# Attention stage of a hybrid encoder: values loaded with a unit's scores, first loads by halves of the channels, branch products from the first tail slot on

## The chip, the cores and the metric

The kernel runs on one core of one Trainium2 chip. What is compared is the device time of one execution in microseconds. TensorE is called PE in the profile, VectorE DVE, ScalarE ACT, GpSimd POOL, SyncE SP; PEld is TensorE's load of the stationary operand.

## What is computed

One pre-norm encoder layer over two inputs: 2048 tokens of a sample and 1024 tokens of a prompt, 1024 channels, fp32.

```python
h = _rms_norm(x, norm_g)
qkv_a, z_a, qkv_b, z_b, beta, alpha, gate_a, gate_b = jnp.split(h @ w_in, split_points, -1)
q_a, k_a = _rms_norm(q_a, q_norm_g), _rms_norm(k_a, k_norm_g)
o_a = _neighbourhood_attention(q_a, k_a, v_a, rpb) * jax.nn.silu(z_a)   # 8 heads of 64
o_b = _deltanet_branch(qkv_b, z_b, beta, alpha, ...)                    # 4 heads of 128
merged = sigmoid(gate_a) * (o_a @ w_branch_a) + sigmoid(gate_b) * (o_b @ w_branch_b)
return x + merged @ w_out
```

The attention is two-dimensional: a token sits on a grid 64 wide, and attends to a window of 8 rows by 16 columns, with a learned bias by relative position. The DeltaNet branch is a chunked recurrent scan in both directions.

## The kernel before, in words

Most products are made in fp16 by splitting each fp32 operand into a high and a low half (`whi`, `wlo`, `rh`, `rl`, `ph`, `pl`) and adding three products (or, where the values `vw` hold both halves, two).

*DeltaNet stage* (`deltanet`, to about 1717 us). All projections but those of q, k and v of the attention are made here, as a filler of 128x256 fp16 products between the steps of the scan. The work goes slot by slot: `step_slot` runs the scan's steps and lets `fill(u)` add filler products until TensorE's count in this slot, `T.cost`, reaches a quarter, a half, three quarters and all of `UNITS`; a 256-wide fp16 product counts 1. At the end the last chunk's outputs are stored (`obd<-P`).

*Attention stage* (to about 2342 us). Its first loads are the weights `w.hi`, `w.lo` of the first pair of heads and the normalised tokens `H[4]` (tiles `rh4`, `rl4`, in two halves of the tokens), from DRAM tiles that the first stage wrote; `load_H` loads a block. Four pairs of heads follow one another; each has six blocks of 512 tokens (two of the prompt, 4 and 5, then four of the sample), and each block four slots. In a slot, `slot(mm)` interleaves a projection of 128 tokens (24 products `ppn`, 128x384, made piece by piece through `work(n, mm)`, with the pieces of `PW`) with one unit of the attention, which is 128 queries by 12 or 16 rows of keys. A unit goes through the slots as a pipeline:

- `unit_bias`: every fourth unit loads the bias `bt` by eight loads for each head (`bias_tile`; POOL's memset comes first).
- `unit_scores` at the end of slot n: products `pS`; DVE adds `bt` and takes the maximum (`Sb`). `unit_exp` follows on ACT in slot n+1.
- `unit_transpose` and `unit_low` in slot n+2, for each of two heads: transposes `pT`, high half `ph` on ACT, low half `pl` on DVE. For the first head the values `vw` are loaded here, by three or four DMAs of 64 KB out of `w.vd`, a DRAM tile; there are two buffers of `vw`.
- `unit_values` in slot n+3: products `pon` out of `vw`, `ph` and `pl`; then `unit_out` on ACT and `unit_sum` on DVE.
- after four units `block_out`: transposes `pO`, gate `otn`, store `oad`.

The projection's values go the other way: `proj_parts` makes `vt`, `norm` stores it to `w.vd` (`vd<-vt`), and `proj_tr` transposes q and k (`pqk`) and writes the high and low halves of the keys, `kh` and `kl`, one tile for the sample (2048 keys) and one for the prompt (1024, two buffers).

*Tail* (13 slots, 2342 to 2432). The projections are over and the last units run. From its second slot on the filler of `slot` is `two_chunks`: the products of two chunks of the branch outputs with the branch weights, `py_` (128x256, 24 of them to one PSUM tile, tag "g", two buffers), made by `merged`. `gated` (DVE, `th<-th,py`) frees the PSUM tile; `split` makes the halves `mm`. `begin` sets up a chunk by six steps in later slots (its second argument gives the slot of each): loads, scaling, `x` times `z` on POOL (the step "act" is next after the load; the steps are `dma`, `act`, `dve2`, `pe`, `dve2`, `dve2`), and so on. What is left of the two chunks is made by `run_merged` when the tail is over.

*Output stage* (to 2876 us). The other chunks' `py_` and the output products `po_`.

What sets the order: in the attention stage and the tail TensorE, DVE and ACT run in the order of the program text (`Pinned`, `PIN = 7`). The order on SP, which issues all loads and stores one after the other, and on POOL is the planner's: it takes the instruction that its model finds ready, by priorities that come from the order in which the program emits them. An instruction that waits holds up what is behind it on its engine. All operations carry line 61, a helper; so they are told apart by the names of their tiles.

Of the kernel before, what the change touches and what calls it, by code (L numbers as in the profile page):

```python
# [45 lines left out]
def emit(nc, tc, x_prompt, x_sample, norm_g, w_in, attn_q_norm_g, attn_k_norm_g, attn_rpb, dn_conv_w, dn_a_log,  # L46
# [120 lines left out]
    def deltanet():  # L167

        SLOTS, UNITS, MOST, FIRST, LAST = 7, 34.0, 3000, (0, 4), (3, 5)
        sm = opn("sm", bufs=4)
        dcp = opn("dcp")
        wdp = opn("wdp", bufs=8)
# [1326 lines left out]
    def proj_tr(w, b, t2):  # L1501

        pt = ps_Q.tile([128, 2, 256], F32, name="pqk", tag="Q")
        for j in range(2):
            x = w.sq.pop(0)
            TP.transpose(pt[:, 0].rearrange("p (b r c) -> p r b c", b=4, r=4)[:, 2 * j:2 * j + 2], x[:, 0:128], ident)
            TP.transpose(pt[:, 1, 128 * j:128 * j + 128], x[:, 128:256], ident)

        if t2 == 0:
            w.q[b] = tuple(nk.tile([128, BLK], F16, name=n, bufs=5) for n in ("qh", "ql"))  # L1510
        sq = 0 if b < 4 else 1
        if sq not in w.k:
            w.k[sq] = tuple(nk.tile([128, (2048, 1024)[sq]], F16, name=f"{n}{sq}", bufs=(1, 2)[sq]) for n in ("kh", "kl"))
        qh, ql = w.q[b]
        kh, kl = w.k[sq]
        qv = lambda t: t.rearrange("p (b r) -> p b r", b=4)[:, :, 64 * t2:64 * t2 + 64]
        pq_ = pt[:, 0].rearrange("p (b r) -> p b r", b=4)
        bs = slice(BLK * (b - 4 * sq) + 256 * t2, BLK * (b - 4 * sq) + 256 * t2 + 256)

        def high():  # L1520
            SP.activation(qv(qh), pq_, AF.Identity, scale=gg)
            SP.activation(kh[:, bs], pt[:, 1], AF.Copy)

        def low():
            VP.scalar_tensor_tensor(qv(ql), in0=pq_, scalar=gg, in1=qv(qh), op0=MUL, op1=SUB)
            VP.tensor_tensor(kl[:, bs], pt[:, 1], kh[:, bs], op=SUB)
            nonlocal done
            done += 1

        at(0, "act2", high)  # L1530
        at(0, "dve2", low)
# [8 lines left out]
    def unit_scores(u):  # L1540


        w, b, cb = u.w, u.b, u.cb
        rt = types[b]
        u.nr = 16 if rt == 1 else 12
        u.kr = row0[b] - (0 if rt == 0 else 4)
        u.kc = min(max(16 * cb - 8, 0), 32)
        if cb == 0:
            w.Os = wk.tile([128, 4, 128], F32, name="Os")
        u.Os = w.Os  # L1550
        rows0, N = 32 * (b // 4), 32 * u.nr
        qg, kg = w.q[b], [t.rearrange("p (r c) -> p r c", c=64) for t in w.k[b // 4]]
        pS = [ps_S.tile([128, 512], F32, name="pS", tag="S") for _ in range(2)]
        for n, (a, c) in enumerate(((0, 0), (0, 1), (1, 0))):
            for hd in range(2):
                hs = slice(64 * hd, 64 * hd + 64)
                TP.matmul(pS[hd][:, 0:N], qg[a][hs, 128 * cb:128 * cb + 128],
                          kg[c][hs, u.kr - rows0:u.kr - rows0 + u.nr, u.kc:u.kc + 32], start=(n == 0), stop=(n == 2))
        u.Sb = [wk.tile([128, 512], F32, name="Sb", bufs=SBB) for _ in range(2)]
        mx = sm.tile([128, 2], F32, name="mx")  # L1560
        for hd in range(2):
            VP.tensor_tensor_reduce(out=u.Sb[hd][:, 0:N], in0=pS[hd][:, 0:N], in1=w.bts[hd][:, (0, 1, 1, 2)[cb], :], scale=1.0,
                                    scalar=-3e38, op0=ADD, op1=MAX, accum_out=mx[:, hd:hd + 1])
        u.nm = sm.tile([128, 2], F32, name="nm")
        VP.tensor_tensor(u.nm, mx, npq.to_broadcast([128, 2]), op=MUL)
# [8 lines left out]
    def unit_transpose(u, hd):  # L1574

        w, N = u.w, 32 * u.nr
        if hd == 0:
            u.vw = wk.tile([128, 4, 256], F16, name="vw")
            for j in range(u.nr // 4):
                SY.dma_start(u.vw[:, j, :], w.vd[u.kr + 4 * j:u.kr + 4 * j + 4, u.kc:u.kc + 32, :])  # L1580
            u.ph = [wk.tile([128, 512], F16, name="ph", bufs=PHB) for _ in range(2)]
            u.pl = [wk.tile([128, 512], F16, name="pl", bufs=PHB) for _ in range(2)]
            u.pT = [None, None]
# [68 lines left out]
                SY.dma_start(H[b][i][:, :, HB * j:HB * j + HB], hdr[b][:, i, j])  # L1652

    w = pair(0)
    for i, t in enumerate((w.hi, w.lo)):
        SY.dma_start(t.rearrange("p j k c -> p (j k c)"), wt0[:, 3072 * i:3072 * i + 3072])
    w.p = [abp[:, 4 + j:5 + j] for j in range(3)]
    pair_scales(w, V)
    load_H(4)
    load_H(5)  # L1660

    order = [10, 11, 8, 9, 0, 1, 2, 3, 4, 5, 6, 7]
# [243 lines left out]
    for hp_ in range(4):  # L1906
# [5 lines left out]
        for b, ats in ((4, ()), (5, (5, 4)), (0, ()), (1, (0,)), (2, (1,)), (3, (2, 3))):  # L1912
            if hp_ == 3 and b == 0:
                branch_weights(0)
            for t in range(4):
                if hp_ == 3 and b == 2 and t == 2:
                    begin(order[0], (0, 2, 3, 4, 4, 5))
                mm = proj_mm(w, b, t)
                slot(mm)
                work(1, mm)  # L1920
# [7 lines left out]
                    units.append((sn + LA, u))  # L1928
    close(p_mm)
    p_g, ps_g = pool("p_g", bufs=2, side="right", space=PSUM)  # L1930
    begin(order[1], (0, 2, 4, 5, 5, 6))

    def two_chunks():
        yield from merged(cs_[0], nwm)
        yield from merged(cs_[1], wkm)

# [2 lines left out]
    while units or B or C or later:  # L1939
        if ws is None and done == 48:  # L1940
            early()
        if n == 11:
            begin(order[2], (0, 2))
        slot(filler if n else iter(()))
        n += 1
    while stk:
        close(stk.pop())
# [67 lines left out]
```

## Time and profile before

| | us |
|---|---|
| three runs | 2873.61, 2874.6, 2876.13 |
| median | 2874.6 |
| the profiled execution | 2877.91 |
| its span | 2876.1 |
| busy: PE, PEld, DVE, ACT, POOL | 2714.3, 2159.7, 1794.1, 1397.0, 890.1 |

In all views times are microseconds from the start of the span. "Busy" is the time in which an engine executes; a bracket behind an instruction gives the idle time ahead of it on its engine and what ended it. A wait for several things is put down to the one that came last by the profile; where the named one has been done for long, it was another, often a load. The clock column is the granted clock of TensorE as a share of 2.4 GHz. SPq is SyncE's issue of a DMA.

### The profile page before, as it was taken

The page shows a single profiled execution, that of the slowest core. Times are in us where ns is not written, and L with a number is a line of the kernel's source. Part 1 is how long each engine was busy: PE and PEld are TensorE (multiplying, and loading weights), DVE is VectorE, ACT ScalarE, POOL GpSimd, SP SyncE. Part 2 cuts the span into 40 slices and gives each one's busy share as a digit, 9 for nine tenths or more (in the row PEclk, how much of TensorE's full clock was granted, in tenths as well). Part 3 has the DMA queues.
Part 4 walks back from the last instruction along what each step waited for, and adds up shares of the span by engine and source line. Part 5 has one row for each costly group of instructions (what it writes and reads, how often), then busy time and mean ns, then how long its engine had stood idle before and what let it go on. Part 6 is the DMA issues. An engine that isn't in the chain of part 4 may idle for free. (4 is left out here: it accounts for less than half of the span.)

```text
span 2876.1 us, 64811 instructions
## 1 busy us (share of the span) xinstructions
PE 2714.3 (94%) x24902; PEld 2159.7 (75%) x24902; DVE 1794.1 (62%) x4266; ACT 1397.0 (49%) x3861; POOL 890.1 (31%) x1545
## 2 busy tenths in 40 slices
PE   7889999989899999999999989999999988999999
PEld 6778888978788878888788885666666656666675
DVE  7567767577574758746666523566666657556654
ACT  4445455555445545555455543666666654212211
POOL 2222111221111212112212215445444433554543
PEclk9899999999999999999999999999999989999999
DMA  7433443344532443232435747333333454543341
GB/s 255 131 112 91 120 122 86 108 128 129 131 105 83 134 135 110 81 89 71 134 106 164 201 138 202 110 102 92 103 90 93 136 191 163 199 147 130 133 155 66
DMA packets 486931, 364.97 MB, mean 127 GB/s; under 512 B 144227, under 2 KB 449247, under 8 KB 485727
## 3 DMA queue, kind: packets, MB, share of 16 engines
q1 hardware_dynamic: 486623, 360.84, 42.0%
q8 instruction: 196, 3.21, 0.5%
q14 instruction: 112, 0.92, 0.1%
HBM read 262.53 MB, written 98.20 MB: 125 GB/s over the span
## 5 line engine op out<-in xcount | busy, mean ns | idle before, releaser
L61 PE MATMUL pp<-hh,w 128*128 128x256 f16 x6912 | 1214.2, 276 | 21.7 <-DVE thz L61 10.1
L61 PEld LDWEIGHTS <-w 128*128 128x128 f16 x10368 | 1021.8, 99 | 159.0 <-issue 16.9
L61 PE MATMUL pp<-hl,w 128*128 128x256 f16 x3456 | 955.5, 276 | 1.7 <-DMA hl<-hdr 1.1
L61 PE MATMUL ppn<-whi,rh 128*128 128x384 f16 x768 | 253.5, 330 | 5.6 <-DMA rh<-hdr 5.6
L61 PEld LDWEIGHTS <-y 128*128 128x128 f16 x2304 | 225.6, 99 | 43.6 <-DVE th L61 8.7
L61 PE MATMUL ppn<-whi,rl 128*128 128x384 f16 x768 | 253.8, 331 | 0.7 <-DMA rl<-hdr 0.7
L61 PE MATMUL ppn<-wlo,rh 128*128 128x384 f16 x768 | 253.1, 330 | 0.0
L61 PEld LDWEIGHTS <-rh 128*128 128x128 f16 x1536 | 146.0, 99 | 77.0 <-issue 9.3
L61 ACT ACTIVATE thz<-pp,wfc 128x256 f32<-128x256 f32 x288 | 124.3, 472 | 158.3 <-PE pp L61 110.0
L61 POOL TENSOR_TENSOR th<-th 128x128 f32<-128x128 f32 (+1 forms) x240 | 149.0, 638 | 165.0 <-DVE th L61 146.7
L61 PEld LDWEIGHTS <-mm 128*128 128x128 f16 x1008 | 98.6, 98 | 115.2
L61 ACT ACTIVATE mm<-th 128x256 f16<-128x256 f32 x144 | 59.1, 446 | 227.7 <-POOL th L61 223.6
L61 DVE TENSOR_TENSOR pl<-pT,ph 128x384 f16<-128x384 f32 (+1 forms) x192 | 111.0, 599 | 88.6 <-ACT ph L61 87.6
L61 DVE CUSTOM_DVE_ANT_0 Sb<-pS,bt 128x384 f32<-128x384 f32 (+1 forms) x192 | 108.9, 599 | 74.8 <-PE pS L61 32.2
L61 ACT ACTIVATE vn<-pk,nbeg 128x128 f32<-128x128 f32 x176 | 64.8, 368 | 171.0 <-PE pk L61 169.9
L61 POOL TENSOR_TENSOR rqk<-rqk,mhalf 128x4 f32<-128x4 f32 x48 | 51.1, 1065 | 305.6 <-DVE rqk L61 303.3
L61 DVE SCALAR_TENSOR_TENSOR S<-S,egl,pk 128x128 f32<-128x128 f32 x160 | 54.8, 343 | 137.5 <-PE pk L61 113.2
L61 ACT ACTIVATE Sb<-Sb,nm,pq 128x384 f32<-128x384 f32 (+1 forms) x192 | 140.0, 733 | 0.4 <-DVE nm L61 0.3
L61 ACT ACTIVATE Os<-pon,rsn 128x64 f32<-128x64 f32 x192 | 49.9, 311 | 181.0 <-PE pon L61 181.0
L61 PEld LDWEIGHTS <-rl 128*128 128x128 f16 x768 | 75.7, 99 | 62.2 <-issue 31.8
L61 ACT ACTIVATE raw<-pp,wfc 128x256 f32<-128x256 f32 x144 | 63.1, 474 | 118.1 <-PE pp L61 113.5
L61 DVE TENSOR_REDUCE wm<-wst 128x1 f32<-128x512 f32 (+1 forms) x111 | 82.2, 761 | 60.1 <-DMA wst<-in_w_in 46.8
(619 smaller groups left out, 5631.2 us busy)
## 6 DMA issues: line engine op xcount, KB each, us to landing
wst<-in_w_in SPq DMA_DIRECT2D x124, 256.0 KB
gtd<-thz SPq DMA_DIRECT2D x192, 128.0 KB
hh<-hdr SPq DMA_DIRECT2D x48, 512.0 KB
hl<-hdr SPq DMA_DIRECT2D x48, 512.0 KB
th<-gtd SPq DMA_DIRECT2D x24, 1024.0 KB
vw<-vd SPq DMA_DIRECT2D x320, 64.0 KB
IT<-gd SPq DMA_DIRECT2D x48, 256.0 KB
bt<-ud SPq DMA_DIRECT2D x256, 48.0 KB
```

Source lines behind the costliest of these rows:

```text
L61: i = f(*a, **k)
```

## The change

- `UNITS` goes from 34.0 to 33.5.
- `kh1`, `kl1` (the prompt's keys) have one buffer instead of two, which frees 4 KB in each partition.
- The tile `vw` and its loads move from `unit_transpose` to `unit_scores`, two slots earlier; it has four buffers instead of two.
- The first loads of the attention stage: before, the whole of `w.hi`, then of `w.lo`, then the two token halves of `H[4]`. After, for the first four channel groups `w.hi`, the first token half of `rh4`, `w.lo`, that of `rl4`; then the same for the other four groups; then the second token halves. Six DMAs become ten, and the weights' contiguous runs go from 6 KB to 1 KB.
- `begin` of the first two chunks: (0, 2, ...) becomes (0, 3, ...), (0, 2, 4, 5, 5, 6) becomes (0, 3, 4, 5, 5, 6): the step after the load, `x` times `z`, comes one slot later.
- `two_chunks` gives 7 empty places first (PW[0] + PW[1]), and the first tail slot uses it too; before, that slot had no filler. Of its 24 places 17 are filled, and every later product stands 7 places later in its slot.

```diff
--- before.py
+++ after.py
@@ -168,7 +168,7 @@
 
 
 
-        SLOTS, UNITS, MOST, FIRST, LAST = 7, 34.0, 3000, (0, 4), (3, 5)
+        SLOTS, UNITS, MOST, FIRST, LAST = 7, 33.5, 3000, (0, 4), (3, 5)
         sm = opn("sm", bufs=4)
         dcp = opn("dcp")
         wdp = opn("wdp", bufs=8)
@@ -1510,7 +1510,7 @@
             w.q[b] = tuple(nk.tile([128, BLK], F16, name=n, bufs=5) for n in ("qh", "ql"))
         sq = 0 if b < 4 else 1
         if sq not in w.k:
-            w.k[sq] = tuple(nk.tile([128, (2048, 1024)[sq]], F16, name=f"{n}{sq}", bufs=(1, 2)[sq]) for n in ("kh", "kl"))
+            w.k[sq] = tuple(nk.tile([128, (2048, 1024)[sq]], F16, name=f"{n}{sq}", bufs=1) for n in ("kh", "kl"))
         qh, ql = w.q[b]
         kh, kl = w.k[sq]
         qv = lambda t: t.rearrange("p (b r) -> p b r", b=4)[:, :, 64 * t2:64 * t2 + 64]
@@ -1548,6 +1548,9 @@
         if cb == 0:
             w.Os = wk.tile([128, 4, 128], F32, name="Os")
         u.Os = w.Os
+        u.vw = wk.tile([128, 4, 256], F16, name="vw", bufs=4)
+        for j in range(u.nr // 4):
+            SY.dma_start(u.vw[:, j, :], w.vd[u.kr + 4 * j:u.kr + 4 * j + 4, u.kc:u.kc + 32, :])
         rows0, N = 32 * (b // 4), 32 * u.nr
         qg, kg = w.q[b], [t.rearrange("p (r c) -> p r c", c=64) for t in w.k[b // 4]]
         pS = [ps_S.tile([128, 512], F32, name="pS", tag="S") for _ in range(2)]
@@ -1575,9 +1578,6 @@
 
         w, N = u.w, 32 * u.nr
         if hd == 0:
-            u.vw = wk.tile([128, 4, 256], F16, name="vw")
-            for j in range(u.nr // 4):
-                SY.dma_start(u.vw[:, j, :], w.vd[u.kr + 4 * j:u.kr + 4 * j + 4, u.kc:u.kc + 32, :])
             u.ph = [wk.tile([128, 512], F16, name="ph", bufs=PHB) for _ in range(2)]
             u.pl = [wk.tile([128, 512], F16, name="pl", bufs=PHB) for _ in range(2)]
             u.pT = [None, None]
@@ -1652,11 +1652,15 @@
                 SY.dma_start(H[b][i][:, :, HB * j:HB * j + HB], hdr[b][:, i, j])
 
     w = pair(0)
-    for i, t in enumerate((w.hi, w.lo)):
-        SY.dma_start(t.rearrange("p j k c -> p (j k c)"), wt0[:, 3072 * i:3072 * i + 3072])
+
+    for k in (slice(0, 4), slice(4, 8)):
+        for i, t in enumerate((w.hi, w.lo)):
+            SY.dma_start(t[:, :, k], wt0[:, 3072 * i:3072 * i + 3072].rearrange("p (j k c) -> p j k c", j=3, k=8)[:, :, k])
+            SY.dma_start(H[4][i][:, k, 0:HB], hdr[4][:, i, 0, k])
+    for i in range(2):
+        SY.dma_start(H[4][i][:, :, HB:BLK], hdr[4][:, i, 1])
     w.p = [abp[:, 4 + j:5 + j] for j in range(3)]
     pair_scales(w, V)
-    load_H(4)
     load_H(5)
 
     order = [10, 11, 8, 9, 0, 1, 2, 3, 4, 5, 6, 7]
@@ -1914,7 +1918,7 @@
                 branch_weights(0)
             for t in range(4):
                 if hp_ == 3 and b == 2 and t == 2:
-                    begin(order[0], (0, 2, 3, 4, 4, 5))
+                    begin(order[0], (0, 3, 3, 4, 4, 5))
                 mm = proj_mm(w, b, t)
                 slot(mm)
                 work(1, mm)
@@ -1928,9 +1932,12 @@
                     units.append((sn + LA, u))
     close(p_mm)
     p_g, ps_g = pool("p_g", bufs=2, side="right", space=PSUM)
-    begin(order[1], (0, 2, 4, 5, 5, 6))
+    begin(order[1], (0, 3, 4, 5, 5, 6))
 
     def two_chunks():
+
+        for _ in range(PW[0] + PW[1]):
+            yield
         yield from merged(cs_[0], nwm)
         yield from merged(cs_[1], wkm)
 
@@ -1941,7 +1948,7 @@
             early()
         if n == 11:
             begin(order[2], (0, 2))
-        slot(filler if n else iter(()))
+        slot(filler)
         n += 1
     while stk:
         close(stk.pop())
```

## Rows read from the trace of the kernel before

**Rows 1.** Windows by stage: length; busy PE, PEld, DVE, ACT, POOL; clock, DMA, GB/s.

```profile
60.00:1717.00 1657.00, 1569.93 (x16108) 1388.44 (x16105) 1065.70 (x2479) 846.55 (x2438) 337.86 (x587) 0.98 0.41 119
1717.00:1730.00 13.00, 3.51 (x10) 1.53 (x10) 0.89 (x9) 4.83 (x18) 6.53 (x13) 0.61 0.83 268
1730.00:2342.00 612.00, 590.01 (x4740) 384.37 (x4740) 367.57 (x1148) 385.57 (x1071) 286.55 (x593) 0.98 0.41 117
2342.00:2432.00 90.00, 73.17 (x651) 56.29 (x652) 62.91 (x164) 47.46 (x123) 27.76 (x40) 0.87 0.52 165
2432.00:2876.00 444.00, 438.59 (x3030) 296.54 (x3028) 254.53 (x385) 84.41 (x164) 217.54 (x272) 1.00 0.41 144
```

**Rows 2.** Waits of PE, 1730 to 2342: total us, times, longest.

```profile
PE pqk L61 <- POOL sqn L61: 4.7, 1, 4.7
PE pon L61 <- DVE y L61: 4.0, 1, 4.0
...
PE pon L61 <- DMA vw<-vd: 3.4, 5, 1.0
PE pon L61 <- DVE wps L61: 2.3, 1, 2.3
```

**Rows 3.** Waits of PE in the tail, 2342 to 2432.

```profile
PE pon L61 <- DMA vw<-vd: 3.5, 6, 0.9
PE pO L61 <- DVE kl L61: 3.4, 1, 3.4
PE py__34202 L61 <- DVE th L61: 2.2, 1, 2.2
...
PE py__34644 L61 <- DVE th L61: 0.5, 1, 0.5
```

**Rows 4.** Timelines of SP and PE at 1798: start, length, operation, [idle <- releaser].

```profile
1798.04 3.57 SPq L61 DMA_DIRECT2D bt<-ud  x8
1801.71 1.62 SPq L61 DMA_DIRECT2D vw<-vd  x3
...
1804.82 0.22 PE L61 MATMUL pon<-vw,ph 128*128 128x128 f16 x1 [2.33 <-DVE wps L61]
```

**Rows 5.** Windows behind the gaps, columns as in rows 1.

```profile
1805.00:1812.00 7.00, 5.56 (x29) 3.68 (x27) 1.78 (x12) 3.43 (x9) 0.43 (x1) 0.52 0.39 117
2249.00:2256.00 7.00, 5.39 (x28) 3.77 (x29) 1.50 (x4) 3.19 (x9) 0.43 (x1) 0.52 0.51 146
2348.00:2355.00 7.00, 5.90 (x38) 4.11 (x39) 6.24 (x17) 2.10 (x6) 4.36 (x6) 0.52 1.03 339
2362.00:2368.00 6.00, 5.52 (x32) 4.43 (x31) 1.59 (x4) 2.17 (x5) 0.00 (x0) 0.50 0.66 261
2416.00:2423.00 7.00, 6.07 (x36) 4.74 (x35) 2.58 (x7) 2.77 (x8) 2.05 (x5) 0.51 0.35 102
```

**Rows 6.** Waits of DVE, 1730 to 2342.

```profile
DVE Sb L61 <- DMA vw<-vd: 6.8, 2, 3.5
```

**Rows 7.** Timelines of SP and PE at the first loads of the attention stage.

```profile
1724.09 0.47 SPq L61 DMA_DIRECT2D rh<-hdr  x1
...
1728.63 0.48 PE L61 MATMUL ppn<-whi,rh 128*128 128x384 f16 x1 [5.65 <-DMA rh<-hdr]
```

**Rows 8.** Timeline of PE at the start of the output stage.

```profile
2434.00 2.78 PE L61 MATMUL py__34759<-op,y 128*128 128x256 f16 x24
```

**Rows 9.** Timeline of DVE in the first tail slot.

```profile
2345.76 2.47 DVE L61 SCALAR_TENSOR_TENSOR op<-x,osp,op 128x1024 f16<-128x1024 f32 x2
```

**Rows 10.** Window of the tail, columns as in rows 1.

```profile
2381.00:2416.00 35.00, 27.08 (x269) 20.83 (x266) 28.18 (x76) 19.33 (x49) 10.45 (x13) 0.95 0.53 165
```

**Rows 11.** Timeline of POOL at 2306.

```profile
2306.94 2.35 POOL L61 TENSOR_TENSOR x<-x,z 128x1024 f32<-128x1024 f32 x1 [5.47 <-DMA z<-szd]
```

**Rows 12.** Waits of PE in the DeltaNet stage, 60 to 1717.

```profile
PE pp L61 <- DVE thz L61: 10.1, 3, 4.4
```

**Rows 13.** Chain of waits, 1780 to 1830: start, length, what.

```profile
1793.05 3.88 DMA vd<-vt
```

## The prediction

> **What bounds the kernel now.** I read the time stage by stage first [rows 1]. The DeltaNet stage, up to 1717 us, keeps TensorE busy for 1569.93 of 1657.00 us, so 87 us of it are waits. The attention stage, 1730 to 2342, is busy for 590.01 of 612.00. The tail, 2342 to 2432, has the worst ratio: 73.17 of 90.00, at a mean granted clock of 0.87. The output stage, from 2432 on, is busy for 438.59 of 444 us at 1.00, and nothing in the change touches it. So TensorE is the bound everywhere, and a gain is either one of its waits taken away or time given back that it spent at 1.2 instead of 2.4 GHz.
>
> Next I read TensorE's waits in the two attention stages [rows 2, 3]. In the main part, the value products `pon` wait 3.4 us for `vw` in five places, and two more entries stand for the same thing: 4.0 us put down to DVE `y` and 2.3 us to DVE `wps`. These DVE steps have nothing to do with `pon`; what is late there is the first of three `vw` loads. SP's timeline shows why [rows 4]: eight bias loads `bt` were issued one after the other for 3.57 us, and the three `vw` loads only at 1801.71, 3.1 us before the product of 1804.82 that uses them. The place at 2249 has the same order of SP. The tail has 3.5 us of `vw` waits in six pieces, 3.4 us of `pO` behind DVE, and a chain of `py` waiting for DVE's `th`: 2.2 us the longest, 0.5 the shortest of five, 1.0 + 2.2 + 2.1 + 1.5 + 0.5 = 7.3 in all [rows 3].
>
> Last I read the granted clock behind those waits [rows 5]. After each of the four largest `vw` gaps it is 0.50 to 0.52 (the 1.2 GHz level) for some 6 to 7 us, with TensorE nearly always busy in them. Work done at 0.52 in 5.56 us takes 5.56 x 0.52 = 2.9 at full clock, so a gap costs a second time: 2.7 us (1805), 2.6 (2249), 2.8 (2362), 3.0 (2416).
>
> **Part by part.**
>
> *Values with the scores, four buffers.* No load is added: 320 `vw` loads of 64 KB stay. They are emitted two slots earlier; a slot lasts 612/96 = 6.4 us [rows 1], so they get up to some 13 us more of lead, and four buffers instead of two let the planner use it (with two, a load cannot go out before the product two units back has run). The waits at 1804 and 2249 need some 4 to 5 us more. The bias loads that blocked the way belong to later units, and are now behind this `vw` in the emitted order. In the main stage 3.4 + 4.0 + 2.3 = 9.7 us of waits and 2.7 + 2.6 = 5.3 us at the lower clock should go: 15.0. The lower bound is 8: the softmax step `Sb` on DVE, which reads `bt`, already waits 6.8 us in rows put down to `vw` [rows 6], which is again SP's queue; if `bt` becomes late in `vw`'s place and as much comes back on TensorE, 15.0 - 6.8 = 8.2 are left. In the tail the 3.5 us of `vw` waits go, and 2.8 + 3.0 = 5.8 us at the lower clock; I take only half of the latter, 2.9: the gap of `pO` in the same tail is also followed by 0.52, from 2348 on [rows 5], so gaps that stay may keep the clock down.
>
> *One buffer for the prompt keys.* It frees the memory. The next pair's prompt keys are written at least six slots after the last read of the old ones, as the loops put all attention units on prompt blocks well before the next pair's blocks 4 and 5; 6 x 6.4 = 38 us cover it. Cost nothing; if that cover were gone, one slot of 6.4 us for each of three pairs.
>
> *First loads by halves of the channels.* Now `rh` is issued at 1724.09, behind the stores of the last DeltaNet chunk, and the first `ppn` starts at 1728.63 after 5.65 us idle: 4.54 us for a 512 KB piece together with the weights before it [rows 7]. The halves of 256 KB let twelve products start when a quarter of the bytes is there. What was last, the store's data (ACT P), stays ahead in SP's queue. Four more DMA issues cost about 0.5 us each on SP. The products then run on at the lower clock, so the second half has time to arrive. I take -1.0; bounds -3 (two thirds of 4.54) and +0.7 (four issues, part hidden). The Trainium skill, Perfetto Trace Analysis, section DMA Optimizations, speaks both ways: splitting may let some loads start sooner, and transfers under 2 KB carry much overhead, which would count against weight runs that go from 6 KB to 1 KB. By the first alone the term would be -3, by the second alone +0.7 or worse. No row here prices runs of 1 KB by themselves.
>
> *Branch products from the first tail slot.* 17 of the 24 `py` products of a chunk go into tail slot 0. In the output stage 24 take 2.78 us, 0.116 each [rows 8], so 17 x 0.116 = 2.0 us leave the end. Slot 0 now has 3.4 us waiting for DVE [rows 3] that could hide them, but only in part: the products need `op`, which DVE makes from 2345.76 to 2348.23 [rows 9], so TensorE, in program order, waits for it ahead of the second head's `pT`, and from there a part of the 3.4 us moves rather than goes. I take -0.8 (bounds -2, all hidden, and +0.4, where the 17 products run at half clock, 4.0 us, behind that wait and hide 1.6 of it). All later `py` groups start 7 products later in the slot, behind `pon` and the first `pT`: the `th` step that frees a PSUM bank has some 1.9 us more. All five `th` waits are at most 2.2, so nearly all of the 7.3 could go; but from 2381 to 2416 DVE is busy 28.18 of 35 us [rows 10], against 27.08 of TensorE, so DVE is close behind. Half: -3.6 (bounds 0 and -7.3). The tail together: 3.5 + 2.9 + 0.8 + 3.6 = 10.8, from 3.1 (no clock, no `th`, slot 0 the wrong way) to 18.6.
>
> *`x z` of the chunks one slot later.* In the main stage TensorE waits 4.7 us for `sqn` [rows 2], because POOL ran `x<-x,z` first for 2.35 us after sitting 5.47 us on the load of `z` [rows 11]. POOL's and SP's orders are the planner's, not the emitted one; one slot of later priority may or may not put `ssn` and `sqn` first. I count 0; the other end is -4.7 and about 2.6 of lower clock, as behind the gap at 2249, so -7.3.
>
> *UNITS 33.5.* A slot's fill stops at the first count not below the limit, so only slots whose other work ends in the upper half of a unit lose a product: by the code's counts about a third of some 450, 147 x 0.116 = 17 us of projections moved later. TensorE's sum is the same. If they all fall into the exposed end (9.5 us idle of 13.00 after 1717 [rows 1]), -8. If the re-dealt slots make two new waits of the largest kind of that stage, 4.4 us [rows 12], +8. I take 0, the middle.
>
> *New waits.* Planner and SP order change everywhere; I put 3 us against it (0 to 9, two of the 4.7 us kind [rows 2]).
>
> **Sum.** 15.0 + 3.5 + 2.9 + 1.0 + 0.8 + 3.6 - 3.0 = 23.8 us. The profiled execution took 2877.91 us (span 2876.1), 3.3 above the median of 2874.6: 2854.1 in its terms, 2850.8 against the median. I forecast 2851. Taken as independent, the distances to the bounds give a root of squares of 15 on the one side (7, 8, 1.7, 8 and 6) and 14 on the other (8, 2, 8, 3 and 7.3), so its own range is 2837 to 2866.
>
> **Rivals.**
> (a) *The gain is given back in half*: `bt` becomes the late load, and the tail goes over to DVE. For it: DVE's 28.18 of 35 [rows 10] and Sb's waits [rows 6]. Main stage 8.2, tail 3.1, first loads 1.0, less 3.0: 9.3 us, 2865.
>
> (b) *The `x z` step works too*: 2851 - 7.3 = 2844. For it: the order of POOL at 2306 is the whole cause [rows 11]; against it: the later chunk step is only a priority.
>
> (c) *The load isn't moved by the planner*: SP already hoists, and `vw` stays behind `bt`. Then only the tail's 3.6 + 0.8 and 1.0 are left, less new waits 3.0: 2872. Against it: the buffers are a hard limit on hoisting, and they are lifted.
>
> (d) *Slower: SP stands still behind its own store.* `vd` is stored and read again as `vw`; in the chain a store's landing took 3.88 us [rows 13]. Emitted with the scores, the first unit of a block comes right behind that store, and SP, which works in order, would hold back `bt`, `rh` and the stores behind it. There are 24 such groups (four pairs, six blocks). If one of them reaches TensorE, it costs what the two gaps of this kind did on the mean, 2.3 and 4.0 with some 0.7 of the 3.4 us each, 3.8, and 2.7 of lower clock: 6.5. From the fifth group on the change loses (26.8 before new waits, 6.5 each); with six: 39 - 26.8 = +12, 2887. Against it: the product is three slots behind, 19 us, and 3.88 fits in that several times; it needs a second load that is late already. The Trainium skill, DMA: Bandwidth & Descriptors, section Anatomy of one DMA — SWDGE (gpsimd) path, says most of a DMA's fixed cost of about 2 us is the receipt of the write, heaviest for HBM; by that figure the hold would be about 2 us a group (an estimate), and the row shows more.
>
> **How the numbers follow.** Forecast 0.49, (a) 0.20, (b) 0.15, (c) 0.08, (d) 0.08. A measurement of this kernel tells about 0.2% or 5.7 us, so "faster" is under 2868.9. Forecast, (b) and most of (a), 0.16, are faster: 0.80. The rest of (a) and (c) are within: 0.12. (d) is slower: 0.08. The range that leaves out no more than two in ten takes (a) and (b) with their spread: 2830 to 2871.
>
> **What would show it.** Right: no `pon` waiting for `vw` in 1730 to 2432, `vw` issued ahead of the eight `bt` at 1798 and 2242, clock 1.0 in the stretches of rows 5, tail under 82 us, `py` waits under 4 us, the DeltaNet stage within 8 us of 1717. Wrong: Sb waiting for `bt` with `pT` late behind it; a longer wait of SP on `vd`; DVE over 85% busy in the tail; a DeltaNet stage longer by over 8 us, which would mean that the third of the slots was set by the scan and not by the fill.

## The result, and the profile after

The changed kernel takes 2854.68 us (median of four runs, 2852.56 to 2857.41) against 2875.03 of the kernel before on the same chip: a ratio of 0.993, 95% interval 0.9913 to 0.9947. On another chip, where the kernel before stood at 2881.54, it took 2851.64, 0.9895 (0.988 to 0.991). The two intervals do not meet, so from chip to chip the ratio differs by more than its interval says. The forecast was 2851, a ratio of 0.9918, with 2830 to 2871 around it. The profiled execution took 2857.41 us, its span is 2855.6.

Windows by stage of the changed kernel, to be laid beside [rows 1] (columns: start:end, length, busy PE, PEld, DVE, ACT, POOL, granted clock, DMA share, GB/s):

```profile
60.00:1717.00 1657.00, 1563.82 (x16082) 1384.37 (x16080) 1065.63 (x2482) 847.56 (x2430) 342.14 (x589) 0.98 0.41 118
1717.00:1732.00 15.00, 6.47 (x46) 4.52 (x44) 0.90 (x9) 6.44 (x27) 6.16 (x13) 0.78 0.51 159
1732.00:2335.00 603.00, 585.12 (x4742) 380.92 (x4742) 366.53 (x1148) 385.44 (x1070) 287.40 (x594) 0.99 0.43 122
2335.00:2411.70 76.70, 66.36 (x670) 52.83 (x670) 62.84 (x165) 48.09 (x124) 29.18 (x42) 0.98 0.60 188
2411.70:2855.60 443.90, 437.31 (x3012) 294.77 (x3010) 243.11 (x384) 84.69 (x164) 220.19 (x271) 1.00 0.41 144
```

The reader sees the tail: 76.70 us at a clock of 0.98 where there were 90.00 at 0.87. Its end is set here where `py` changes over to the work behind the tail, so lengths of stages are better taken between marks that both traces have. There are four: the last `pp` (end of the DeltaNet stage's projections), the 97th `ppn` (four slots into the attention stage), the last `ppn`, and the first `po`.

| us, one profiled execution each | last `pp` at | to 97th `ppn` | to last `ppn` | to first `po` | to the end |
|---|---|---|---|---|---|
| before | 1714.0 | 33.6 | 594.1 | 100.3 | 434.2 |
| after | 1720.8 | 31.6 | 582.4 | 84.8 | 436.0 |
| difference | +6.9 | -2.0 | -11.7 | -15.5 | +1.8 |

The differences add up to the -20.5 us between the spans. The last `pp` is not quite the same place in the two kernels: with `UNITS` at 33.5 some 1 us of the scan's last products stands ahead of it instead of behind it, so about 1 us of the first column belongs to the second.

What the tail's 15.5 us are made of shows in the windows from the last `ppn` to the first `po`, first of the kernel before, then of the changed one:

```profile
2341.61:2441.86 100.25, 83.36 (x743) 65.11 (x742) 69.51 (x176) 50.09 (x130) 34.88 (x50) 0.88 0.55 180
2334.80:2419.57 84.77, 74.43 (x743) 59.89 (x742) 67.16 (x175) 51.71 (x133) 33.76 (x50) 0.98 0.61 198
```

The same 743 products take 8.9 us less, at a mean clock of 0.98 instead of 0.88, and TensorE's idle time falls from 16.9 to 10.3 us, 6.6 less. From the 97th to the last `ppn` the same reading gives 572.23 us busy before and 565.68 after, and 21.8 and 16.7 us idle: 6.6 and 5.0 less.

TensorE's waits between 1732 and 2335 of the changed kernel, beside [rows 2] (total us, times, longest):

```profile
PE ppn L61 <- DMA rl<-hdr: 8.0, 2, 7.6
PE pqk L61 <- POOL sqn L61: 5.8, 1, 5.8
PE pO L61 <- DVE kl L61: 5.4, 9, 0.7
```

No `pon` waits for `vw` any more, and the lines for `y` and `wps` are gone: the 9.7 us of [rows 2]. The wait for `sqn` is still there, 5.8 instead of 4.7, and `pO` and `pm` wait a little more than before (`pm` 3.3, where it was 2.1; `pO` 5.4, where it was 3.7). In the tail, beside [rows 3]:

```profile
PE pon L61 <- ACT ph L61: 2.3, 2, 1.3
PE py__33541 L61 <- ACT qs L61: 1.5, 1, 1.5
PE pqk L61 <- POOL sqn L61: 1.4, 1, 1.4
```

Neither `vw` nor the chain of `py` waiting for `th` is there; the 7.3 us of that chain went completely. So did the 3.4 us of `pO` waiting for DVE's `kl`. SP's queue shows the cause in the main stage, beside [rows 4]:

```profile
1782.62 7.44 SPq L61 DMA_DIRECT2D vw<-vd  x11
...
1800.38 0.52 SPq L61 DMA_DIRECT2D vw<-vd  x1
1800.94 8.51 SPq L61 DMA_DIRECT2D bt<-ud  x16
1809.55 0.37 SPq L61 DMA_DIRECT2D vd<-vt  x1
1810.01 2.24 SPq L61 DMA_DIRECT2D vw<-vd  x4
```

Eleven loads of `vw` go out from 1782.62 on, one more at 1800.38, and the bias loads, now 16 in a row for 8.51 us, come behind them. The clock, beside [rows 5]:

```profile
1752.39:2300.00 547.61, 536.68 (x4418) 352.28 (x4417) 346.58 (x1089) 362.11 (x1008) 262.34 (x544) 1.00 0.41 117
2306.00:2309.00 3.00, 2.77 (x12) 1.13 (x13) 0.01 (x1) 0.75 (x2) 2.67 (x7) 0.50 0.15 45
2340.00:2355.00 15.00, 13.28 (x121) 10.38 (x121) 12.80 (x31) 7.71 (x20) 6.70 (x9) 0.89 0.95 307
2355.00:2411.00 56.00, 50.49 (x528) 40.67 (x527) 46.01 (x123) 35.45 (x90) 19.34 (x28) 1.00 0.51 160
```

From 1752 to 2300 the clock is 1.00: no gap in it is followed by the 1.2 GHz level. Behind the wait for `sqn`, from 2306 to 2309, it is 0.50. In the tail it is 0.89 from 2340 to 2355 and 1.00 from there to 2411.

### The profile page after: what moved, and what is told of

Same layout as the page of the kernel before. It is cut to its first block, busy times and chain, and to the rows that moved or that the text cites. A ratio compares the mean times of both kernels' runs of the same rounds, so it can differ in the third digit from the quotient of the medians.

```text
span 2855.6 us, 64795 instructions
## 1 busy us (share of the span) xinstructions
PE 2698.4 (94%) x24902; PEld 2150.1 (75%) x24902; DVE 1781.1 (62%) x4266; ACT 1399.5 (49%) x3861; POOL 898.0 (31%) x1545
## 4 chain that ended last, share of the span: by engine, by line
PE 64%; DVE 13%; DMA 8%; SPq 4%; ACT 4%; POOL 3%; issue 3%; DVEq 0%; POOLq 0%; ACTq 0%
PE pp L61 27%; PE ppn L61 9%; PE pk L61 5%; SPq L61 4%; DVE YT L61 3%; DVE P L61 2%; PE pT L61 2%; PE pS L61 2%; PE lv L61 2%; DMA wst<-in_w_in 1%; PE pon L61 1%; DMA z<-szd 1%; PE gq L61 1%; DMA IT<-gd 1%; ACT P L61 1%
## 5 line engine op out<-in xcount | busy, mean ns | idle before, releaser
L61 PEld LDWEIGHTS <-y 128*128 128x128 f16 x2304 | 224.1, 98 | 36.8 <-issue 9.2
L61 DVE CUSTOM_DVE_ANT_0 Sb<-pS,bt 128x384 f32<-128x384 f32 (+1 forms) x192 | 108.9, 599 | 73.3 <-PE pS L61 31.6
```

The source lines that it names most:

```text
L61: i = f(*a, **k)
```

## The experiments

Each run is a kernel beside the kernel before on one chip. The DeltaNet stage differs by chance by several us from one execution to the next (below), so most verdicts are read from the lengths of the other stages, in the marks of the table above. All of them:

| us, one profiled execution each | last `pp` at | to 97th `ppn` | to last `ppn` | to first `po` | to the end | ratio to before (95%) |
|---|---|---|---|---|---|---|
| `vw_alone` | 1714.2 | 34.5 | 584.3 | 92.9 | 434.2 | 0.9925 (0.9908, 0.9942) |
| `tail_alone` | 1722.8 | 34.4 | 595.2 | 97.0 | 436.0 | 0.9990 (0.9974, 1.0006) |
| `units_alone` | 1714.9 | 34.1 | 591.9 | 100.2 | 433.8 | 0.9988 (0.9976, 1.0001) |
| `loads_alone` | 1713.2 | 33.2 | 593.1 | 100.2 | 434.2 | 0.9989 (0.9977, 1.0002) |
| `vw_tail` | 1714.3 | 34.4 | 581.6 | 84.1 | 436.1 | 0.9913 (0.9893, 0.9932) |
| `vw_bufs` | 1715.2 | 34.0 | 590.8 | 93.9 | 434.4 | 0.9963 (0.9952, 0.9975) |
| `vw_early2` | 1715.5 | 35.0 | 596.9 | 97.0 | 434.4 | 0.9993 (0.9982, 1.0005) |
| `after_xz` | 1717.4 | 30.9 | 578.3 | 85.0 | 434.3 | 0.9889 (0.9868, 0.9909) |
| `after_again` | 1711.5 | 30.3 | 582.6 | 84.8 | 435.2 | 0.9895 (0.9880, 0.9910) |
| `two_xz` | 1713.4 | 33.5 | 575.5 | 88.9 | 434.6 | 0.9877 (0.9863, 0.9891) |
| `units34_xz` | 1721.3 | 33.3 | 577.0 | 84.2 | 434.8 | 0.9874 (0.9859, 0.9889) |
| `xz_alone` | 1717.0 | 33.2 | 593.6 | 99.1 | 434.1 | 0.9998 (0.9986, 1.0009) |

The first four ran on one chip, the next four on a second, the last four on a third. How far single executions can be trusted shows where kernels share a stage's edits. The five in which the values' loads are as before (before, `tail_alone`, `units_alone`, `loads_alone`, `xz_alone`) have 591.9 to 595.2 from the 97th to the last `ppn`; in the tail the kernel before, `units_alone` and `loads_alone` have 100.2 to 100.3, and `vw_tail`, both executions of the changed kernel, `after_xz` and `units34_xz` have 84.1 to 85.0.

### One part at a time

*The values alone.*

```diff
-            w.k[sq] = tuple(nk.tile([128, (2048, 1024)[sq]], F16, name=f"{n}{sq}", bufs=(1, 2)[sq]) for n in ("kh", "kl"))
+            w.k[sq] = tuple(nk.tile([128, (2048, 1024)[sq]], F16, name=f"{n}{sq}", bufs=1) for n in ("kh", "kl"))
 def unit_scores(u):
...
+        u.vw = wk.tile([128, 4, 256], F16, name="vw", bufs=4)
+        for j in range(u.nr // 4):
+            SY.dma_start(u.vw[:, j, :], w.vd[u.kr + 4 * j:u.kr + 4 * j + 4, u.kc:u.kc + 32, :])
 def unit_transpose(u, hd):
...
-            u.vw = wk.tile([128, 4, 256], F16, name="vw")
-            for j in range(u.nr // 4):
-                SY.dma_start(u.vw[:, j, :], w.vd[u.kr + 4 * j:u.kr + 4 * j + 4, u.kc:u.kc + 32, :])
```

> Kernel before with the values' loads moved to the scores, four buffers, and one buffer of prompt keys; nothing else. Theory 1 (the values' loads were late behind the bias loads, and being earlier is what brings the gain of the attention stage): 10 to 16 us faster than before, first to last ppn some 602 us instead of 613, no pon waiting for vw, in the tail 3.5 to 6 us less. Rival (the waits only move to the next load unless the other edits come too): under 5 us faster, Sb waiting for bt.

Measured: 0.9925, and 604.0 us from first to last `ppn` (613.0 before). By stage 9.8 us are gone from the main stage and 7.4 from the tail, and no `pon` waits for `vw`. That is theory 1, with more in the tail than was expected; by the medians it is 21.8 us, more than the 10 to 16. But the tail's `py` now wait longer (waits of TensorE, 2333 to 2430):

```profile
PE py__34305 L61 <- DVE th L61: 3.4, 1, 3.4
...
PE py__34211 L61 <- DMA bt<-ud: 2.2, 1, 2.2
```

With four smaller ones for `th` it is 8.4 us where there were 7.3.

*The branch products alone.*

```diff
 def two_chunks():
+    for _ in range(PW[0] + PW[1]):
+        yield
     yield from merged(cs_[0], nwm)
...
-    slot(filler if n else iter(()))
+    slot(filler)
```

> Kernel before with only the branch products in the first tail slot and their shift by seven places. Theory 1 (the shift takes the waits of py for th away, and their lower clock): last ppn to first po 7 to 10 us shorter than the 100.3 of before, the vw waits of the tail (3.5 us) stay. Rival (the 15.5 us of the tail come from the values being there in time): under 4 us.

Measured: 3.3 us off the tail, 1.8 more behind it, and 0.9990 with 1 inside the interval. By the bound of 4 us that is the rival. The `py` waits for `th` are gone as in the changed kernel, but TensorE waits for the values instead (2352 to 2449):

```profile
PE pon L61 <- DMA vw<-vd: 8.1, 9, 2.1
```

8.1 us in nine pieces, where there were 3.5 in six [rows 3]. So each edit takes its own wait away, and much of that time goes to the wait that the other one removes.

*UNITS alone, first loads alone.*

```diff
-SLOTS, UNITS, MOST, FIRST, LAST = 7, 34.0, 3000, (0, 4), (3, 5)
+SLOTS, UNITS, MOST, FIRST, LAST = 7, 33.5, 3000, (0, 4), (3, 5)
```

> Kernel before with UNITS 33.5 only. Theory 1 (the start of the attention stage moved from 1728.6 to 1732.3 because of the re-dealt slots): first ppn 2 to 5 us later than before, whole kernel +2 to +5. Rival (the split loads did it): first ppn at 1728.6 within 1 us, no difference.

Measured: first `ppn` at 1729.0, last `pp` at 1714.9, 0.9988 (to 1.0001): no difference that can be told, and theory 1 falls. The changed kernel's later end of the DeltaNet stage is not the work of `UNITS`: `vw_alone` and `tail_alone`, on one chip, have the order of the kernel before on all five engines up to there, and their last `pp` at 1714.2 and 1722.8; the changed kernel itself, run again, had it at 1711.5. The spread of that stage from one execution to the next covers the whole +6.9.

TensorE's order at the end of the stage did change. Before, it waited 4.42 and 0.73 us for the scan's `P` on ACT, then 5.65 us for the first loads [rows 7]; here projections fill the first of these, and the loads take it back:

```profile
1716.40 2.37 PE L61 MATMUL ptf<-ident,P 128*128 128x128 f32 x8 [1.27 <-ACT P L61]
1728.97 0.48 PE L61 MATMUL ppn<-whi,rh 128*128 128x384 f16 x1 [10.19 <-DMA rh<-hdr]
```

That is 11.5 us where there were 10.8.

```diff
-for i, t in enumerate((w.hi, w.lo)):
-    SY.dma_start(t.rearrange("p j k c -> p (j k c)"), wt0[:, 3072 * i:3072 * i + 3072])
+for k in (slice(0, 4), slice(4, 8)):
+    for i, t in enumerate((w.hi, w.lo)):
+        SY.dma_start(t[:, :, k], wt0[:, 3072 * i:3072 * i + 3072].rearrange("p (j k c) -> p j k c", j=3, k=8)[:, :, k])
+        SY.dma_start(H[4][i][:, k, 0:HB], hdr[4][:, i, 0, k])
+for i in range(2):
+    SY.dma_start(H[4][i][:, :, HB:BLK], hdr[4][:, i, 1])
...
-load_H(4)
```

> Kernel before with only the first loads split by halves of the channels. Theory 1 (splitting helps a little, the slots did the harm): first ppn 0.5 to 2 us earlier than 1728.6, whole kernel -1. Rival (ten loads with runs of 1 KB are slower or come later in the queue): first ppn 2 to 4 us later, whole kernel +2 to +4.

Measured: the first `ppn` at 1722.29, 6.3 us earlier than before (5.5 counted from the last `pp`), far more than theory 1 had; but at the 97th `ppn` only 0.4 us of it is left (33.2 against 33.6), and the kernels without this edit spread from 33.2 to 35.0 there. SP's timeline and TensorE's show both:

```profile
1716.78 0.49 SPq L61 DMA_DIRECT2D rh<-hdr  x1
...
1722.30 1.01 SPq L61 DMA_DIRECT2D obd<-P  x2
...
1723.87 0.54 SPq L61 DMA_DIRECT2D rh<-hdr  x1
```

```profile
1720.88 1.35 PE L61 MATMUL ptf<-ident,P 128*128 128x128 f32 x4 [0.72 <-ACT P L61]
1722.29 0.48 PE L61 MATMUL ppn<-whi,rh 128*128 128x384 f16 x1
...
1728.49 0.50 PE L61 MATMUL ppn<-whi,rh 128*128 128x384 f16 x1 [2.86 <-DMA rh<-hdr]
```

The first halves were issued at 1716, ahead of the last stores `obd`, and TensorE went on from `ptf` without a gap. The second halves came behind those stores, at 1723; TensorE waited 2.86, 0.69 and 0.40 us for them. What was gained at the start was lost at the second half. In the changed kernel the planner put the first half of the tokens behind the stores too (1726.19), and a gap stayed:

```profile
1720.84 0.27 PE L61 MATMUL pp<-hh,w 128*128 128x256 f16 x1
1722.38 2.37 PE L61 MATMUL ptf<-ident,P 128*128 128x128 f32 x8 [1.27 <-ACT P L61]
1732.30 0.48 PE L61 MATMUL ppn<-whi,rh 128*128 128x384 f16 x1 [7.55 <-DMA rl<-hdr]
```

Beside the 10.19 us of `units_alone`, which has the same order on TensorE there, the split takes 2.6 us off this wait. To the 97th `ppn` `units_alone` has 34.1 and the three executions with both edits (`after`, `after_again`, `after_xz`) 30.3 to 31.6; with the split alone (`loads_alone`, `units34_xz`) it is 33.2 and 33.3. So the split, too, may be worth more beside another edit, some 3 us; no whole time shows it.

### Together: does one edit hand its gain to the other?

> Kernel before with two edits: the values' loads early with four buffers, and the branch products from the first tail slot. Alone, from last ppn to first po, the one took 7.4 us off the 100.3 and the other 3.3; the changed kernel has 84.8, 15.5 off. Theory 1 (each edit alone only hands its gain to the wait that the other one removes, so together they give more than the sum): 84 to 87 us. Rival (the remaining 4.8 us come from the x z step or from a chance in one execution): 89 to 91 us. Whole kernel: 22 to 26 us faster than before by the first, 17 to 20 by the second.

Its edit is the sum of the first two diffs. Measured: 84.1 us from last `ppn` to first `po`, 16.2 off, where the two alone had 7.4 + 3.3 = 10.7; the ratio is 0.9913, not to be told from that of the whole change (0.993 and 0.9895 on two chips). Theory 1 holds, by the tail. TensorE's idle time in that stretch shows the handing on: 16.9 us before (19.4 in `units_alone` and `loads_alone`, whose tail is the same), 15.5 in `vw_alone`, 18.0 in `tail_alone`, 8.2 here. What the single edits gained was mostly time at the lower clock: the busy time is 77.4 and 79.1 us, against 83.4 before (80.8 in `units_alone` and `loads_alone`). The whole times alone could not show it: by the medians 21.8 and 4.9 us singly and 25.3 together, each with some 5 us to either side. These two edits are all of the change that shows in the whole time.

### Place or buffers?

```diff
-u.vw = wk.tile([128, 4, 256], F16, name="vw")
+u.vw = wk.tile([128, 4, 256], F16, name="vw", bufs=4)
```

> Kernel before with four buffers of values (and one of prompt keys), but the loads left at the transposes. Theory 1 (the planner hoists loads as far as the buffers let it, so the buffers are the edit that counts): first to last ppn 602 to 606 us as with both. Rival (the place in the program decides, since it gives the load its priority ahead of later bias loads): 611 to 614 us, vw issued behind the eight bt as before.

(One buffer of prompt keys goes with it.) Measured: 610.0 us from first to last `ppn`, between the two expectations and nearer to the rival's (590.8 from the 97th on, where the kernels without early values have 591.9 to 595.2), but 0.9963: a gain of 0.4%, clear of its interval. At 1794 SP still has twelve `bt` ahead of `vw`, and `pon` waits nearly as before (7.5 us in the main stage, 9.7 before); the second timeline is TensorE's:

```profile
1794.63 8.12 SPq L61 DMA_DIRECT2D bt<-ud  x12
1802.79 1.62 SPq L61 DMA_DIRECT2D vw<-vd  x3
```

```profile
1805.91 0.22 PE L61 MATMUL pon<-vw,ph 128*128 128x128 f16 x1 [2.28 <-DVE wps L61]
```

Most of the gain is the tail's 6.4 us (93.9), almost all of the 7.4 that both halves of the edit had there.

```diff
 def unit_scores(u):
...
+        u.vw = wk.tile([128, 4, 256], F16, name="vw")
+        for j in range(u.nr // 4):
+            SY.dma_start(u.vw[:, j, :], w.vd[u.kr + 4 * j:u.kr + 4 * j + 4, u.kc:u.kc + 32, :])
```

> Kernel before with the values' loads at the scores, but two buffers. Theory 1 (buffers count): 611 to 614 us from first to last ppn, since a load still can't go before the product two units back; perhaps worse, since SP then stands waiting for that product with bt behind it. Rival (the place counts): 602 to 606 us.

(And away from `unit_transpose`.) Measured: 616.9, 3.9 us longer than before (596.9 from the 97th on, 2.8 longer); 0.9993 on the whole. Theory 1's "perhaps worse" came true in that stage. `pon` no longer waits for `vw` there, but TensorE waits for DVE, and DVE for loads (waits of TensorE, then of DVE):

```profile
PE pqk L61 <- DVE wm L61: 11.5, 7, 2.0
```

```profile
DVE Sb L61 <- DMA vw<-vd: 35.6, 7, 7.8
DVE Sb L61 <- DMA bt<-ud: 23.8, 5, 5.0
```

`Sb` reads the bias `bt`, not `vw`; the names `vw`, `bt` and `vd` in these rows stand for one wait, that for the bias loads (see rival (d) below). Together they are 66.5 us, against 27.4 before. SP's timeline has `vw` between the first and the other seven bias loads of a head:

```profile
1961.73 0.32 SPq L61 DMA_DIRECT2D bt<-ud  x1
1962.14 1.64 SPq L61 DMA_DIRECT2D vw<-vd  x3
1963.82 3.29 SPq L61 DMA_DIRECT2D bt<-ud  x7
```

The reason that theory 1 gave, SP standing at a `vw` whose buffer the product two units back still holds, isn't shown: SP's waits put down to `pon` are 60.3 us, and 65.7 before. Its waits put down to the store `oad` grew, from 1.9 to 24.0 us. So what is shown is the order: with two buffers the early place puts `vw` among the `bt`, and these come late; with four buffers the same waits of `Sb` are 24.1 to 36.8 us in the runs that have both. In the main stage neither half brings much without the other.

### The wait that stayed

In the changed kernel POOL still sits on the load of `z` and runs `x<-x,z` ahead of `ssn`, as in [rows 11]:

```profile
2301.33 2.35 POOL L61 TENSOR_TENSOR x<-x,z 128x1024 f32<-128x1024 f32 x1 [6.62 <-DMA z<-szd]
2303.63 0.20 POOL L61 TENSOR_TENSOR ssn<-ssn,frow 128x4 f32<-128x4 f32 x1
```

The experiment lets POOL start that product only behind the last `sqn` product emitted before it:

```diff
-            G.tensor_tensor(sq, qs[:, 0:256].rearrange("p (a b) -> p a b", a=4),
+            anchors["pool"] = G.tensor_tensor(sq, qs[:, 0:256].rearrange("p (a b) -> p a b", a=4),
                             ss[:, :, None].to_broadcast([128, 4, 64]), op=MUL)
...
-    G.tensor_tensor(x[:, 1], x[:, 1], z, op=MUL)
+    with tc.issue_after(anchors["pool"].ins):
+        G.tensor_tensor(x[:, 1], x[:, 1], z, op=MUL)
```

> Changed kernel, and POOL may start the product x z of a chunk only after the last sqn product that was emitted before it. The changed kernel still has 5.8 us of TensorE waiting for sqn at 2306 behind it. Theory 1 (POOL's order is the cause, the one-slot shift of the change didn't alter it): that wait is gone, 5 to 8 us less than the changed kernel between first and last ppn (595 to 598 instead of 602.5). Rival (sqn is late for another reason, or the wait moves to DVE's om): 601 to 603 us.

Measured: 599.0 from first to last `ppn`, 3.5 less than the changed kernel, short of the 5 to 8 and outside both ranges; from the 97th on it is 578.3 instead of 582.4, 4.1 us less. POOL's timeline:

```profile
2307.07 0.61 POOL L61 TENSOR_TENSOR sqn<-qs,ssn 128x256 f32<-128x256 f32 x1
2307.64 2.36 POOL L61 TENSOR_TENSOR x<-x,z 128x1024 f32<-128x1024 f32 x1
```

`x<-x,z` runs without a wait right behind `sqn`, and TensorE's wait for `sqn` is gone from the list; in its place 2.1 us of `pqk` waiting for DVE's `om` are new. So theory 1 is right in its cause and too high in size, and a part of the gain went to the step behind.

> The kernel before with only POOL's product x z held back behind the last sqn product. Theory 1 (the wait for sqn costs its 4.7 us and some 2.6 at the lower clock behind it, whatever else is in the kernel): first to last ppn 606 to 609 instead of 613, whole kernel -4 to -7, 0.9975 to 0.9985. Rival (without early values the time is only lost to the next vw wait): 611 to 613.

The same edit in the kernel before. Measured: 593.6 from the 97th to the last `ppn` (594.1 before), 0.9998: the rival. The wait for `sqn` is gone there too, but SP issued the next `vw` at 2313.53, no earlier than before (2312.64), and the second timeline, TensorE's, shows what comes of it:

```profile
2313.53 1.80 SPq L61 DMA_DIRECT2D vw<-vd  x3
```

```profile
2315.38 0.22 PE L61 MATMUL pon<-vw,ph 128*128 128x128 f16 x1 [3.88 <-DMA vw<-vd]
```

The late `vw` had been hidden behind the wait for `sqn`. The same edit is worth 4 to 6 us of the main stage with the values early, and nothing without.

> The changed kernel once more, beside the three below on the same chip. Theory 1 (of the change only the values' loads and the branch products bring anything that can be measured): a ratio of 0.991 to 0.993 to the kernel before, as the two edits alone had (0.9913). First ppn at 1722 to 1733, as chance in the DeltaNet stage has it; first to last ppn 601 to 603, last ppn to first po 84 to 85.

Measured: 0.9895; 602.1, and 84.8. As expected, with a first `ppn` at the early end, 1722.3, but for a ratio below the 0.991 to 0.993.

> The two edits alone (values early with four buffers, branch products from the first tail slot) and POOL's product x z held back behind the last sqn product; UNITS, first loads and the slots of begin as before. Theory 1 (the remaining three edits bring 1 to 2 us at most): within 3 us of the next run; first ppn about 14.5 us after the last pp, against 10 to 12 with the split loads; first to last ppn 595 to 599. Rival (UNITS 33.5 is worth something in the DeltaNet stage): 4 us or more slower than the changed kernel with the same addition, 0.9889.

Measured: 0.9877, so the rival falls; by the medians 3.4 us behind the next run, a little over the 3 of theory 1. The main stage is the shortest of all (575.5 from the 97th on), but the tail is 88.9 instead of 84 to 85. There TensorE waits for DVE, and DVE for the bias loads:

```profile
PE pS L61 <- DVE mx L61: 3.9, 1, 3.9
```

```profile
2375.94 0.56 DVE L61 CUSTOM_DVE_ANT_0 Sb<-pS,bt 128x384 f32<-128x384 f32 x1 [5.35 <-DMA bt<-ud]
```

The wait of 3.9 us is 0.8 in the changed kernel. Why these loads are late is open. `begin` still had the slots of the kernel before, (0, 2, ...), and the first loads were as before. These alone don't do it, as `vw_tail`, which has them without the hold, is at 84.1; nor does the hold with the slots and loads of the change, as `units34_xz` is at 84.2.

> The changed kernel with UNITS back at 34.0 and POOL's product x z held back. Theory 1 (UNITS makes no difference): 0.988 to 0.990 of the kernel before, as with 33.5 (0.9889). Rival: above 0.991, the DeltaNet stage (last pp) later by 4 us or more than in the other runs of this chip.

The changed kernel with the hold and `UNITS` at 34.0. Measured: 0.9874 (0.9859 to 0.9889), with 33.5 it was 0.9889 on another chip (0.9868 to 0.9909). No difference from `UNITS` in the whole time, as by theory 1. The last `pp` is the latest of the four on this chip, 1721.3, which the rival had as its sign; but the profiled execution is the slowest of its four (2852.39, the median is 2844.47). On this chip the changed kernel without the hold had 0.9895: the hold is worth some 0.2%, with intervals that overlap. `two_xz` and this one have the lowest ratios of the study.

## Why the prediction was right, step by step

*Values with the scores: right, in mechanism and size.* The terms were -15.0 for the main stage and +3.0 for new waits, so -12; measured are -11.7. The parts fit too: 5.3 at the lower clock and 9.7 less 3.0 of waits were forecast, TensorE's busy time fell by 6.6 and its idle time by 5.0. The new waits are there too: `sqn` 5.8 instead of 4.7, `pO` 5.4 instead of 3.7, more of `pm`. The reading that 4.0 us "for `y`" and 2.3 us "for `wps`" were late loads is borne out: both lines vanish with the loads' place (`vw_alone`), and the second stays with the buffers alone (`vw_bufs`), behind the twelve `bt`. That four buffers "let the planner use" the lead was half of it; `vw_bufs` shows that without the place they change little in the main stage.

*The tail: right in its causes, too small, and by the clock.* Forecast 10.8, measured 15.5, and 1.8 of it given back behind the first `po`. The forecast had 2.9 of clock and 7.9 of waits (3.5 + 0.8 + 3.6); TensorE's busy time fell by 8.9 and its idle time by 6.6. The clock term counted two low stretches and halved them, out of caution, and left out the one behind `pO` [rows 5]; in the changed kernel only the 15 us from 2340 on are below 1.00. The waits came out a little under the forecast: those for `th` went whole (7.3, where 3.6 were taken) and `pO`'s 3.4 went too, but new ones came, the longest 1.5 for ACT `qs` and 1.4 for `sqn`. DVE, whose nearness was the reason for halving `th`, is busy 62.84 of 76.70 us, 82%, and was not the bound. That the two edits need each other there (7.4 and 3.3 alone, 16.2 together) was not in the forecast, which added their terms; as both were made, the sum did not suffer by it.

*First loads: right in sign, not told from nothing.* Forecast -1.0; measured -2.0 in the changed kernel, with some 1 us of it due to the mark, and -0.4 alone, within the spread. The prediction had the stores staying ahead of the loads; alone, the first half went ahead of them, and TensorE started 6.3 us earlier, and the second half then cost nearly all of it. The Trainium skill, Perfetto Trace Analysis, section DMA Optimizations, says that splitting may allow some DMAs to start sooner; the start agrees (1722.29 against 1728.63), the end of the stretch gained 0.4. The overhead of small runs isn't told apart here.

*One buffer for the prompt keys, counted at 0:* no run has it by itself. ACT, which writes `kh`, has no wait for it in the list of the changed kernel.

*Branch products in slot 0:* `py` waits there 1.5 us for ACT `qs` and 0.4 for `op`, so the wait for `op` that was forecast came, behind one that wasn't.

*`x z` one slot later, counted at 0:* right. POOL's order didn't follow the emitted one; the wait is there, 5.8 us. The other end of -7.3 was not far off as a price of the hold (4.1 in the changed kernel).

*UNITS, counted at 0:* right within what chance does to that stage (1711.5 to 1722.8 for the last `pp`). The -8 at one end had a real wait in view, and most of it went (`units_alone`); but the wait for the first loads behind it grew by as much.

*Rivals.* (a) did not come: DVE did not take the tail over, and `Sb`'s waits for its bias loads grew only from 27.4 to 30.0 us. (b) did not come, as POOL's order stayed, nor (c), as `vw` goes out ahead of the `bt`. (d), SP standing behind its own store, did not come either, though a row of DVE looks like it (waits of DVE, 1732 to 2335):

```profile
DVE Sb L61 <- DMA vd<-vt: 23.6, 9, 3.3
```

There were 10.1 us in four under that name before. But `Sb` doesn't read `vd`. Each of the nine waits ends 2 to 3 us after the last of eight `bt` loads was issued, and the store goes out right behind these eight, so that its landing falls in the same moment. One of them, beside SP's lines at 1800.94 and 1809.55 above:

```profile
1811.33 0.56 DVE L61 CUSTOM_DVE_ANT_0 Sb<-pS,bt 128x384 f32<-128x384 f32 x1 [3.23 <-DMA vd<-vt]
```

So the rows that name `bt`, `vd` and `vw` are one wait: 10.5 + 10.1 + 6.8 = 27.4 us before, 2.8 + 23.6 + 3.6 = 30.0 after. The prediction had read 6.8 of it [rows 6] as the whole, and its price for (a) rests on that part alone. SP, for its part, issues `vw` at 1810.01, right behind that store; none of its own waits in the stage is put down to the store `vd<-vt`, and the longest put down to any DMA is 1.4 us. No run here shows the hold for which the prediction cites the Trainium skill (DMA: Bandwidth & Descriptors, section Anatomy of one DMA — SWDGE (gpsimd) path); that section is about DMAs issued by GpSimd, and these are SyncE's.

*The total.* 23.8 us forecast, 20.4 measured by the medians, 20.5 in the profiled executions: -11.7 and -2.0 as forecast or better, -15.5 better by 4.7, +1.8 behind the tail not foreseen, and +6.9 of chance in the DeltaNet stage. Without that chance it would be some 27; on the other chip the difference of the medians was 29.9. So that the forecast of 2851 came within 4 us is in part luck: a tail forecast too low and a slow DeltaNet stage work against each other. Of the +1.8, 0.9 are waits of `py` for DVE in the output stage (2.0 us, 1.1 before). What the rest is stays open: every kernel with the branch products in slot 0 and without the hold on POOL had 435.2 to 436.1 there, those without the branch products 433.8 to 434.4.

## What to carry to other kernels

A wait that the profile puts down to an engine that has nothing to do with it (`y`, `wps`) may be a load: look in the queue's timeline at what was issued ahead of it. The name of a DMA can mislead in the same way, as `vd` and `vw` did for `Sb`: ask what the waiting instruction reads. A late load needs both an earlier place and the buffers for it; here the one without the other brought little or nothing in the main stage. Waits in a row hide each other: the one removed alone hands its time to the next, so an edit may look worthless by itself (0.999) and be worth something beside another; test them together before dropping one. And read single executions by stage, between marks that both traces have, if one stage differs by chance by more than the effect.

## What the runs showed of the hardware

Six of the kernels have one and the same order on all five engines up to the end of the DeltaNet stage (before, `vw_alone`, `tail_alone`, `vw_bufs`, `vw_early2`, `xz_alone`); it ended between 1714.0 and 1722.8 us in their executions, and on one and the same chip at 1714.2 (`vw_alone`) and 1722.8 (`tail_alone`). The changed kernel ended it at 1720.8 and 1711.5. The forecast had taken the stage for one that repeats, and charged its whole uncertainty to `UNITS`. And how long the lower clock lasts behind a gap is not fixed by the gap: behind the same wait of 5.8 us for `sqn` it was 0.50 for 3 us in one execution of the changed kernel, and in the other, `after_again`, for 6.8 (2293.0 to 2299.8). Behind the gaps of before it was 6 to 7 us at 0.50 to 0.52 [rows 5].
